# A fourth staging buffer for weights, and gates that keep the scaled projection in the place of their result

## The chip, the cores and the metric

The kernel runs on one core of a Trainium2 chip. The core has five engines that work side by side, each through its own instructions in order: TensorE (PE in the profile; its weight loads are shown apart as PEld), VectorE (DVE), ScalarE (ACT), GpSimd (POOL) and SyncE (SP, which here only issues transfers). The metric is the device time of one execution in microseconds. Three runs of the kernel before took 1794.14, 1794.47 and 1795.31 us; their median is 1794.47.

## The reference

The kernel computes two layers of a decoder trunk on 512 tokens of width 2048, in float32. A layer normalises its input, multiplies it by one wide matrix, runs three groups of heads on the parts of the product, gates each with a SiLU, and multiplies the result by an output matrix, onto the residual.

```
def _layer(x, norm_g, w_in, ..., w_out):
    h = _rmsnorm(x, norm_g)
    proj = h @ w_in                      # 2048 x 7696
    (cv_h, cv_b, cv_c, cv_g, sb_q, sb_k, sb_v, sb_g,
     gl_q, gl_k, gl_v, gl_g, gl_lr) = split(proj)
    y_conv = cv_b * (conv3(cv_c * cv_h) + bias) * silu(cv_g)          # 512 columns
    y_sb   = stick_breaking(rms(sb_q), rms(sb_k), sb_v) * silu(sb_g)  # 8 heads of 128
    g      = log_sigmoid(gl_lr @ gla_w_up + gla_b_up) / 16
    y_gla  = rms(gla(gl_q, gl_k, gl_v, g)) * silu(gl_g)               # 4 heads
    return x + concat(y_conv, y_sb, y_gla) @ w_out                    # 2048 x 2048
```

`stick_breaking` is a causal attention of which the weights come from sums of log-sigmoids over the keys; `gla` is a linear attention whose state decays by a gate that depends on the data.

## The kernel before

**Weights in blocks.** Both matrices are cut into blocks of 256 columns (one has 16 columns more, the low-rank part). There are 38 blocks a layer: 30 of `w_in`, then 8 of `w_out`. The list `specs` has them in the order of use. Each block is loaded in two halves of 1024 rows (the contraction dimension). A half goes through these steps:

- `fetch` (L295): SyncE issues a 1 MB transfer into a staging tile of the pool `stage`, which has three buffers. For the block with the low-rank part there is a second, small transfer.
- `wmax` (L306): ScalarE squares the staged half and sums it, for a bound on its size. The squares go into a scratch tile, `junk`.
- `wscale` (L313 to L329), once for a block: GpSimd adds the two halves' sums over the partitions, and VectorE makes a power of two of them.
- `whi` (L343): ScalarE writes the scaled half as float16, the high part, into the tile `wh` of the pool `wpool`, three buffers.
- `wlo` (L350): VectorE writes what the high part left over, also in float16, into `wl`. It is the last reader of the staging tile, so its end gives the buffer back.

A projection is three products of float16 parts: high times high, high times low and low times high. There are three forms. `project_cols` (L507 to L509) puts columns on the partitions, 96 matmuls of 128x512. `project_toks` (L515 to L517) puts tokens there, 192 matmuls of 128x256. `project_by_token` (L540) does one group of tokens after another, each with all high parts first and the low part of the weights last; it is used where each group of tokens is wanted by itself, at the two ends of a layer. A projection writes two of the three PSUM banks of the pool `psp`.

**Order of the work.** In a layer: the values of the linear attention (blocks 0 and 1, by token), its query and key, its two gates, the first convolution half (four blocks, of which the third is its gate), four rounds of attention heads (value, gate, query, key), the second convolution half, and the output projection. The linear attention's levels (L673 to L723) and its output (L766 to L798) run beside the convolution's and the first attention round's projections. An attention round's scores and values are put into a list, `later`, and taken out of it between the projections of the next round: the weights of the heads (tile `za`) are turned by transposing transfers (L911, issued by SyncE) into the tile `th`, and L927 multiplies them by the values.

The program is traced in this order, with the loads of the next block (`load`, called by `weights` for the block in use and the one after) at a higher priority. A planner then orders the instructions of each engine by an estimated timeline, and gives out the buffers of the pools as they come free in it. So a load is placed where its staging buffer is free in that timeline, however early that is. At the start of the kernel the order on VectorE and ScalarE is written out by hand.

**The gates.** `gate` (L546 to L560) makes a SiLU of two PSUM banks, one after the other. ScalarE copies the scaled bank (L550) into the scratch tile `gy`, of which there is one; then comes a chain of ScalarE and VectorE steps on a second scratch tile `ga` (L552 to L556, two buffers); and VectorE multiplies both into the gate's tile `g` (L557). `g` has two buffers. They go to the two gates of the linear attention (last read at L798), the two of the convolution and the four of the attention rounds (last read at L934); at the end of layer 0 also to the gain of the next norm.

Two more places use `gy`: the column numbers `colno` in the startup (L107 to L124), and a scratch tile `r_` of the decay (L624 to L626).

Of the kernel before, what the change touches and what calls it, by code (L numbers as in the profile page):

```python
# [11 lines left out]
ALU = mybir.AluOpType  # L12
# [5 lines left out]
P = 128  # L18
# [16 lines left out]
def hybrid_trunk(ctx, tc, x, norm_g, w_in, conv_w, conv_b, sb_qn_g, sb_kn_g,  # L35
                 gla_w_up, gla_b_up, gla_on_g, w_out, out):
    nc = tc.nc
    V, S, G, T = nc.vector, nc.scalar, nc.gpsimd, nc.tensor
    depth, D = norm_g.shape
    seq = x.shape[1]  # L40
# [6 lines left out]
    NG = D // GW  # L47

    const = ctx.enter_context(tc.tile_pool(name="const", bufs=1))
    stage = ctx.enter_context(tc.tile_pool(name="stage", bufs=3))  # L50
    wpool = ctx.enter_context(tc.tile_pool(name="wpool", bufs=3))
    big = ctx.enter_context(tc.tile_pool(name="big", bufs=4))
    work = ctx.enter_context(tc.tile_pool(name="work", bufs=2))
# [8 lines left out]
    def nm(s):  # L62
        uid[0] += 1
        return f"{s}_{uid[0]}"
# [4 lines left out]
    def wk(shape, tag, bufs=None, dt=F32):  # L69
        return work.tile(shape, dt, tag=tag, name=nm(tag), bufs=bufs)  # L70
# [4 lines left out]
    def bank(pool, tag):  # L75
        return pool.tile([P, 512], F32, tag=tag, name=nm("ps" + tag))
# [27 lines left out]
    epst = const.tile([P, 1], F32, tag="epst", name="epst")  # L104
    V.memset(epst, EPS)

    colno = wk([P, P], "gy", 1)  # L107
    V.tensor_tensor_scan(colno, ones.to_broadcast([P, P]), ones.to_broadcast([P, P]), -1.0, ALU.mult, ALU.add)
    parno = wk([P, 32], "raw", 1)
    V.transpose(parno, colno[:, :32])  # L110
# [380 lines left out]
    for l in range(depth):  # L491
# [53 lines left out]
        def gate(ps, u, mx=None):  # L545

            g = wk([P, 2, seq], "g")
            for c in range(2):
                y = wk([P, seq], "gy", 1)
                S.activation(y, ps[c], AF.Copy, scale=u)  # L550
                a = wk([P, seq], "ga")
                S.activation(a, y, AF.Abs)  # L552
                S.activation(a, a, AF.Exp, scale=-1.0)
                S.activation(a, a, AF.Ln, bias=1.0)
                V.scalar_tensor_tensor(a, y, 0.0, a, ALU.min, ALU.subtract)
                S.activation(a, a, AF.Exp)  # L556
                V.tensor_tensor(g[:, c, :], y, a, ALU.mult)  # L557
            if mx is not None:
                V.tensor_reduce(mx, g, AX.XY, ALU.max, apply_absolute_value=True)
            return g  # L560
# [55 lines left out]
        for p in range(2):  # L616
            gp = bank(psm, "m")
            T.matmul(gp, wup[:, p * P:(p + 1) * P], lrT, start=True, stop=True)
            bcol = par[:, base["bu"] + 2 * l + p:base["bu"] + 2 * l + p + 1]
            a = wk([P, seq], "ga")  # L620
            S.activation(a, gp, AF.Abs, bias=bcol)
            S.activation(a, a, AF.Exp, scale=-1.0)
            S.activation(a, a, AF.Ln, bias=1.0)
            r_ = wk([P, seq], "gy", 1)  # L624
            S.activation(r_, gp, AF.Relu, bias=nbu[:, l, p:p + 1], scale=-1.0)
            V.tensor_tensor(a, a, r_, ALU.add)  # L626
            for t in range(NT):
                ts_ = slice(t * P, (t + 1) * P)
                V.tensor_tensor_scan(Pc[:, p, ts_], ones.to_broadcast([P, P]), a[:, ts_], 0.0, ALU.mult, ALU.add)
# [32 lines left out]
        for p in range(2):  # L662
            ps, u = project_cols()
            gmx = sm(1, "ggm")
            gg.append(gate(ps, u, gmx))
            m = sm(1, "gb")
            V.tensor_tensor(m, gmx, onmax[:, l:l + 1], ALU.mult)
            gsc.append(mixscale(6 + p, m, "g"))
# [23 lines left out]
        for p in range(2):  # L692
# [88 lines left out]
            for hh in range(2):  # L781
# [8 lines left out]
                r_ = wk([P, seq], "e")  # L790
# [46 lines left out]
        def conv_out(j, y, then=lambda: None):  # L837

            ps, u = project_cols()
            g = gate(ps, u)  # L840
            V.tensor_tensor(y, y, g, ALU.mult)
            bound = sm(2, "cm")

            def limit(m):
                V.tensor_reduce(m, y, AX.XY, ALU.max, apply_absolute_value=True)
                return m

            then()
            if j:

                V.tensor_scalar(bound[:, 1:2], limit(bound[:, 0:1]), loaded[cursor[0]][1], 2.0 ** 29, ALU.mult, ALU.mult)
                s_ = mixscale(j, bound[:, 1:2], "c", 14.0)
                weight_ratio()
            ps, u = project_cols()
            for c in range(2):
                V.scalar_tensor_tensor(y[:, c, :], ps[c], u, y[:, c, :], ALU.mult, ALU.mult)
            if not j:
                s_ = mixscale(j, limit(bound[:, 0:1]), "c")
            for c in range(2):
                mixsplit(2 * j + c, y[:, c, :], s_)  # L860
# [80 lines left out]
        for j in range(4):  # L941
# [14 lines left out]
            go()  # L956
            ps, u = project_cols()
            g = gate(ps, u, bm[:, 1:2])
            gm = allmax(bm[:, 0:1], 1, "b")
            m = sm(1, "sbm")  # L960
# [109 lines left out]
```

## Time and profile before

| | |
|---|---|
| median of three runs | 1794.47 us |
| the profiled execution | 1794.15 us |
| its span in the profile | 1792.4 us |
| TensorE busy | 1746.4 us, 97% of the span |
| ScalarE busy | 1090.8 us, 61% |
| VectorE busy | 1040.0 us, 58% |
| mean granted TensorE clock | 0.997 |
| weights and other data moved | 202.62 MB, 113 GB/s |

All times within the profile are microseconds from the start of the span. A row of the timeline has the start, the duration, the engine (SPq is SyncE's queue), the line, the operation, the tiles written and read, and in brackets the idle time of the engine before it and who ended it. A row of waits has the engine and line that waited and the one waited for; then the sum in us, the number of times and the longest. A row of windows has the stretch and its length, then busy time and number of instructions of PE, PEld, DVE, ACT and POOL (fewer columns where one line alone is asked for), the granted clock as a share of full speed, the DMA engines' busy share and the GB/s they moved. A row of transfers has the tiles, the queue, the kind, the number, the size of each, and the median time from issue to landing. The ends of matmuls are modelled, so that a busy TensorE is not one at its peak.

### The profile page before, as it was taken

The page shows a single profiled execution, that of the slowest core. Times are in us where ns is not written, and L with a number is a line of the kernel's source. Part 1 is how long each engine was busy: PE and PEld are TensorE (multiplying, and loading weights), DVE is VectorE, ACT ScalarE, POOL GpSimd, SP SyncE. Part 2 cuts the span into 40 slices and gives each one's busy share as a digit, 9 for nine tenths or more (in the row PEclk, how much of TensorE's full clock was granted, in tenths as well). Part 3 has the DMA queues.
Part 4 walks back from the last instruction along what each step waited for, and adds up shares of the span by engine and source line. Part 5 has one row for each costly group of instructions (what it writes and reads, how often), then busy time and mean ns, then how long its engine had stood idle before and what let it go on. Part 6 is the DMA issues. An engine that isn't in the chain of part 4 may idle for free. (4 is left out here: it accounts for less than half of the span.)

```text
span 1792.4 us, 30839 instructions
## 1 busy us (share of the span) xinstructions
PE 1746.4 (97%) x12880; PEld 1238.9 (69%) x12880; DVE 1040.0 (58%) x1977; ACT 1090.8 (61%) x1655; POOL 54.9 (3%) x105
## 2 busy tenths in 40 slices
PE   7999999999999999999999999999999999999999
PEld 5744446777778764788886444568686878548888
DVE  5466777656565656533464575876666566564333
ACT  8557566667575766555554675665666666665431
POOL 1000000000000000000010000000000000000000
PEclk9999999999999999999999999999999999999999
DMA  6322222243535344454423232223444534444441
GB/s 216 118 95 94 71 94 72 92 121 86 141 102 133 109 128 115 143 178 142 134 82 118 94 93 73 80 86 83 132 111 114 128 107 124 119 123 142 142 142 48
DMA packets 257676, 202.62 MB, mean 113 GB/s; under 512 B 84658, under 2 KB 256764, under 8 KB 257024
## 3 DMA queue, kind: packets, MB, share of 16 engines
q1 hardware_dynamic: 248528, 191.19, 37.0%
q10 hardware_dynamic: 9008, 9.45, 1.6%
q8 instruction: 101, 1.65, 0.4%
q14 instruction: 39, 0.32, 0.1%
HBM read 173.36 MB, written 8.39 MB: 101 GB/s over the span
## 5 line engine op out<-in xcount | busy, mean ns | idle before, releaser
L306 ACT ACTIVATE junk<-st 128x2048 uint8<-128x2048 f32 (+1 forms) x152 | 291.0, 1914 | 334.6 <-DMA st<-in_w_in_dram 240.1
L515 PE MATMUL psp<-wh,m 128*128 128x256 f16 x1664 | 453.6, 273 | 2.6 <-DVE raw L981 1.7
L517 PE MATMUL psp<-wh,m 128*128 128x256 f16 x1664 | 453.5, 273 | 0.0
L516 PE MATMUL psp<-wl,m 128*128 128x256 f16 x1664 | 453.5, 273 | 0.0
L350 DVE SCALAR_TENSOR_TENSOR wl<-st,ws,wh 128x2048 f16<-128x2048 f32 (+1 forms) x120 | 282.1, 2353 | 153.3 <-ACT wh L343 145.9
L343 ACT ACTIVATE wh<-st,ws 128x2048 f16<-128x2048 f32 (+1 forms) x120 | 239.8, 2000 | 92.1 <-PE psp L517 58.0
L515 PE MATMUL psp<-wh,x 128*128 128x256 f16 x768 | 209.9, 273 | 2.3 <-DVE raw L981 1.7
L516 PE MATMUL psp<-wl,x 128*128 128x256 f16 x768 | 209.9, 273 | 0.0
L517 PE MATMUL psp<-wh,x 128*128 128x256 f16 x768 | 209.8, 273 | 0.0
L507 PE MATMUL psp<-x,wh 128*128 128x512 f16 x512 | 194.1, 379 | 0.0
L507 PE MATMUL psp<-m,wh 128*128 128x512 f16 x512 | 194.1, 379 | 0.0
L508 PE MATMUL psp<-x,wh 128*128 128x512 f16 x512 | 194.0, 379 | 0.0
L508 PE MATMUL psp<-m,wh 128*128 128x512 f16 x512 | 194.0, 379 | 0.0
L509 PE MATMUL psp<-x,wl 128*128 128x512 f16 x512 | 193.7, 379 | 0.0
L509 PE MATMUL psp<-m,wl 128*128 128x512 f16 x512 | 193.7, 379 | 0.0
L509 PEld LDWEIGHTS <-wl 128*128 128x128 f16 x1024 | 100.2, 98 | 123.0 <-issue 4.4
L508 PEld LDWEIGHTS <-wh 128*128 128x128 f16 x1024 | 100.2, 98 | 117.4 <-issue 2.1
L507 PEld LDWEIGHTS <-wh 128*128 128x128 f16 x1024 | 100.2, 98 | 117.1 <-issue 2.0
L515 PEld LDWEIGHTS <-m 128*128 128x128 f16 x1664 | 162.8, 98 | 23.9 <-DVE raw L981 2.3
L516 PEld LDWEIGHTS <-m 128*128 128x128 f16 x1664 | 162.8, 98 | 20.5 <-issue 1.6
L517 PEld LDWEIGHTS <-m 128*128 128x128 f16 x1664 | 162.8, 98 | 20.1 <-issue 1.4
L316 DVE TENSOR_SCALAR wq<-wgm 128x1 f32<-128x1 f32 x76 | 16.2, 213 | 262.1 <-POOL wgm L313 262.0
(267 smaller groups left out, 2315.9 us busy)
## 6 DMA issues: line engine op xcount, KB each, us to landing
st<-in_w_in_dram SPq DMA_DIRECT2D x120, 1024.0 KB, 5.3
st<-in_w_out_dram SPq DMA_DIRECT2D x32, 1024.0 KB, 5.8
x<-in_x_dram SPq DMA_DIRECT2D x4, 1024.0 KB
qT<-in_x_dram ACTq DMA_DIRECT2D x8, 512.0 KB, 5.1
qT<-xs ACTq DMA_DIRECT2D x8, 512.0 KB
xs<-x SPq DMA_DIRECT2D x14, 256.0 KB, 4.4
out_dram<-kT SPq DMA_DIRECT2D x14, 256.0 KB, 4.3
th<-za SPq DMA_TRANSPOSE x64, 5.5
```

The lines of the kernel that those rows point to most:

```text
L306: S.activation(junk(HK * n).rearrange("p (k n) -> p k n", k=HK), staged[i][h][:, :, :n], AF.Square, accum_out=peak[i][:, h:h + 1])
L316: V.tensor_scalar(m, gm[:, 0:1], gm[:, 1:2], 2.0 ** -120, ALU.add, ALU.max)
L343: S.activation(wh[:, ks, :n], staged[i][h][:, ks, :n], AF.Copy, scale=s_)
L350: V.scalar_tensor_tensor(wl[:, ks, :n], staged[i][h][:, ks, :n], s_, wh[:, ks, :n], ALU.mult, ALU.subtract)
L507: T.matmul(o, wh[:, kk, cs], xh[:, :, k, :], start=st_, stop=False)
L508: T.matmul(o, wh[:, kk, cs], xl[:, :, k, :], start=False, stop=False)
L509: T.matmul(o, wl[:, kk, cs], xh[:, :, k, :], start=False, stop=en)
L515: T.matmul(o, ah[:, t, k, :], wh[:, kk, :n], start=st_, stop=False, skip_group_check=True)
L516: T.matmul(o, ah[:, t, k, :], wl[:, kk, :n], start=False, stop=False, skip_group_check=True)
L517: T.matmul(o, al[:, t, k, :], wh[:, kk, :n], start=False, stop=en, skip_group_check=True)
```

## The change

The pool `stage` gets a fourth buffer. A staging tile is 8 x 272 float32 on each partition, 8704 bytes. The tag `gy` (one tile of 512 float32, 2048 bytes a partition) goes away, and its three users move:

- In `gate` the scaled bank is copied into the half of `g` where the result will stand, and the last product is made in place.
- The column numbers take a buffer of the tag `th`, the turned attention weights.
- The decay's scratch takes a buffer of the tag `za`, the attention weights before they are turned.

```
-    stage = ctx.enter_context(tc.tile_pool(name="stage", bufs=3))
+    stage = ctx.enter_context(tc.tile_pool(name="stage", bufs=4))
...
-    colno = wk([P, P], "gy", 1)
+    colno = wk([P, P], "th", 2)
...
             g = wk([P, 2, seq], "g")
             for c in range(2):
-                y = wk([P, seq], "gy", 1)
+                y = g[:, c, :]
                 S.activation(y, ps[c], AF.Copy, scale=u)
                 a = wk([P, seq], "ga")
...
                 S.activation(a, a, AF.Exp)
-                V.tensor_tensor(g[:, c, :], y, a, ALU.mult)
+                V.tensor_tensor(y, y, a, ALU.mult)
...
-            r_ = wk([P, seq], "gy", 1)
+            r_ = wk([P, seq], "za")
```

## The prediction

> **What bounds the kernel now.** I read the page's first two parts, then TensorE's waits, then every stretch in which TensorE waited, on all engines.
>
> ```profile
> span 1792.4 us, 30839 instructions
> PE 1746.4 (97%) x12880; PEld 1238.9 (69%) x12880; DVE 1040.0 (58%) x1977; ACT 1090.8 (61%) x1655; POOL 54.9 (3%) x105
> ```
> ```profile
> PE psz L688 <- ACT m L682: 5.3, 11, 1.3
> PE psm L927 <- DMA th<-za: 5.0, 6, 2.3
> PE psz L779 <- ACT za L766: 4.9, 4, 1.7
> PE psp L540 <- ACT wh L343: 4.9, 2, 3.4
> ```
> ```profile
> ACT junk L306 <- DMA st<-in_w_in_dram: 240.1, 90, 8.4
> SPq L295 <- DVE wl L350: 831.4, 103, 19.7
> ACT gy L550 <- DVE g L557: 3.9, 2, 2.1
> ```
>
> TensorE is the bound: it is idle for 1792.4 - 1746.4 = 46 us, in waits of which, the startup aside, only one is over 2.3 us. Its weights come late at one line only, L540 (4.9 us, two waits, one of them 3.4). So the 831 us that SyncE spends waiting for a staging slot (L350 frees it) are no loss by themselves. They matter where ScalarE, which works in the order of its queue, stands before a load that has not landed: L306 does so for 240 us. Most of that is idle time that ScalarE has to spare; it costs only where TensorE needs what stands behind it in the queue. The gates' single scratch tile shows in 3.9 us, two waits.
>
> The run that was profiled took 1794.15 us, 1.75 over its span and 0.32 under the median 1794.47; I make the sum against 1794.15 and add 0.32 at the end.
>
> **Fourth staging buffer, at the start of layer 1.** This is the place where a slot is worth time. SyncE, ScalarE, VectorE, TensorE in turn:
>
> ```profile
> 875.24 3.98 SPq L295 DMA_DIRECT2D st<-in_w_in_dram  x3
> 898.14 1.00 SPq L295 DMA_DIRECT2D st<-in_w_in_dram  x2
> 914.89 0.38 SPq L295 DMA_DIRECT2D st<-in_w_in_dram  x1
> 929.78 15.34 SPq L295 DMA_DIRECT2D st<-in_w_in_dram  x3
> ```
> ```profile
> 914.00 1.02 ACT L410 ACTIVATE m<-psz 128x1024 f16<-128x1024 f32 x1 [4.17 <-PE psz L408]
> 916.98 2.02 ACT L306 ACTIVATE junk<-st 128x2176 uint8<-128x2176 f32 x1
> 919.44 2.00 ACT L306 ACTIVATE junk<-st 128x2176 uint8<-128x2176 f32 x1
> 924.59 2.10 ACT L343 ACTIVATE wh<-st,ws 128x2176 f16<-128x2176 f32 x1
> 935.62 1.91 ACT L306 ACTIVATE junk<-st 128x2048 uint8<-128x2048 f32 x1 [5.71 <-DMA st<-in_w_in_dram]
> 937.53 2.09 ACT L343 ACTIVATE wh<-st,ws 128x2176 f16<-128x2176 f32 x1
> ```
> ```profile
> 927.28 2.47 DVE L350 SCALAR_TENSOR_TENSOR wl<-st,ws,wh 128x2176 f16<-128x2176 f32 x1
> ```
> ```profile
> 929.05 5.52 PE L540 MATMUL psp<-wh,m 128*128 128x256 f16 x48 [0.24 <-ACT m L410]
> 935.93 0.38 PE L540 MATMUL psp<-wl,m 128*128 128x256 f16 x2
> 939.67 0.61 PE L540 MATMUL psp<-wh,m 128*128 128x272 f16 x2 [3.35 <-ACT wh L343]
> ```
> ```profile
> 939.70:945.44 5.74, 5.74 (x26) 3.75 (x26) 5.03 (x3) 2.08 (x2) 0.00 (x0) 0.50 0.36 108
> 450.49:453.92 3.43, 2.83 (x13) 1.89 (x14) 2.27 (x4) 1.06 (x1) 0.00 (x0) 0.50 0.90 251
> ```
>
> The second half of block 1's high part (L343 at 937.53) needs a buffer that block 0 last reads in the matmuls ending at 929.05 + 5.52 = 934.57. It starts 937.53 - 934.57 = 3 us later, because a squaring pass (L306 at 935.62) stands ahead of it and waits 5.71 us for a load. That load was issued at 929.78, when L350 (927.28 + 2.47 = 929.75) gave its slot back. TensorE ran out at 935.93 + 0.38 = 936.31 and waited 3.35 us; after that its clock was granted at half for 5.74 us more, 2.87 us of work lost.
>
> With four slots each load takes the slot freed one half earlier. The second half of block 1, issued at 898.14, goes out with the group at 875.24; its squaring passes, at 916.98 and 919.44, fit into ScalarE's 4.17 us of idle time before 914.00 or earlier; the high part at 924.59 and the low part at 927.28 move up with them, and so does the load that they release. The squaring pass that blocked is then done before 934.57, the high part runs from there for 2.09 us to 936.7, and TensorE waits 936.7 - 936.3 = 0.4 us. The gain is 3.35 - 0.4 = 2.95 of wait and 2.87 of clock: **5.8 us**. Ends: 0, if another load takes that place, and 3.35 + 2.87 = 6.2. I take 5.8, since the chain moves up by 921.44 - 914.00 = 7.4 us or more (the end of the second squaring, now and then), and 937.53 - 934.57 = 3 us are needed.
>
> [...]
>
> **Fourth staging buffer, elsewhere.** The same transfers, squarings and conversions are issued, so no work is added or removed. In the steady state the pace of the loads is set by TensorE: it frees a buffer of converted weights, L343 and L350 convert, L350 frees a slot, L295 fetches, L306 squares. A fourth slot moves this row one half ahead and leaves as many squarings behind a fresh load as before. I take 0. The lower end is that the waits at L779 (4.9) and L927 (5.0), where ScalarE had just stood at L306, all go, with the half clock after 450 (3.43 x 0.5 = 1.7): -11.6.
>
> ```profile
> 0.00:44.80 44.80, 34.85 (x202) 24.42 (x203) 26.07 (x82) 37.36 (x44) 7.09 (x12) 1.00 0.65 216
> ```
> ```profile
> st<-in_w_in_dram SPq DMA_DIRECT2D x120, 1024.0 KB, 5.3
> th<-za SPq DMA_TRANSPOSE x64, 5.5
> ```
>
> In the startup, the second half of layer 0's block 1 can now be fetched before the small parameter rows. The slice moved 216 GB/s at 0.65 busy, so 332 when busy, and one half more (1024 KB, 1.05 MB) ahead of the rows is 3.2 us. That is the upper end if TensorE stood still for the transpose of those rows. I take 0, the nearest row being the startup's own order, in which nothing waits for them: the planner puts that transpose where it sees the rows arrive.
>
> **The gates write into their result.** No instruction is added: the same copy and the same product, at other addresses. What changes is waits, and they bind at one gate, that of the first convolution half (layer 0 shown, and one row of layer 1).
>
> ```profile
> 240.01 0.67 ACT L550 ACTIVATE gy<-psp,wu 128x512 f32<-128x512 f32 x1
> 252.02 0.69 ACT L550 ACTIVATE gy<-psp,wu 128x512 f32<-128x512 f32 x1 [2.06 <-DVE g L557]
> 264.66 0.63 ACT L556 ACTIVATE ga<-ga 128x512 f32<-128x512 f32 x1 [2.07 <-DVE ga L555]
> ```
> ```profile
> 247.65 0.74 DVE L798 SCALAR_TENSOR_TENSOR za<-za,par,g 128x512 f32<-128x512 f32 x1
> ```
> ```profile
> 266.39 0.22 PE L688 MATMUL psz<-m 128*128 128x128 f16 x1 [0.51 <-ACT m L682]
> 267.58 0.22 PE L688 MATMUL psz<-m 128*128 128x128 f16 x1 [0.64 <-ACT m L682]
> 1152.51 0.22 PE L688 MATMUL psz<-m 128*128 128x128 f16 x1 [0.52 <-ACT m L682]
> ```
> ```profile
> 248.00:265.06 17.06, 9.10 (x24) 2.32 (x24) 1.00 0.22 67
> ```
>
> Gained: the second copy (252.02) need not wait for the first half's product, so the chain behind it is over before 264.66, where it now holds ScalarE for 2.07 us, and the two waits at 266.39 and 267.58 (1.15 us) may go. Twice, for the same in layer 1 (0.52 at 1152.51 is its first): -2.3. Lost: the first copy (240.01) now needs a gate tile. There are two, and one is read last at 247.65 + 0.74 = 248.39. So the PSUM bank is free at 248.39 + 0.67 = 249.1 instead of 240.7. The next projection (32 matmuls of L507; the last row counts the 24 after its first 8) enters its second bank at 248.0: 1.1 us of wait, 2.2 in two layers. Since ScalarE no longer runs the gate at 240, L798 can also come earlier, and then it is 0. Ends -2.3 and +2.2; I take 0. At the other gates both tiles are long free.
>
> **Index tile and decay scratch.** They move into tags with two buffers of which the first use comes hundreds of us later or earlier; the work that hides them is all of the first projections. 0.
>
> **Sum:** 1794.15 - 5.8 + 0 + 0 = 1788.35, and 0.32 for the median: **1788.7 us**.
>
> **Rivals.**
> 1. *The waits at loads go everywhere.* By -11.6 more: 1777. For it: ScalarE's idle time at L306 stands before the waits at L779 and L927. Against: the pace argument above. [...]
> 2. *The change does not do what it says.* A later load takes the place of the one at 935.62, and the wait stays: 1794.5. Against: the blocks ahead are converted 7 us sooner, and 3 are enough.
> 3. *Transposes queue behind loads: slower.*
>
> ```profile
> 449.48 4.89 SPq L911 DMA_TRANSPOSE th<-za  x3
> ```
>
> Attention's transposes (5.5 us to landing) share SyncE's queue with the loads, and six times TensorE already waits for them at L927. If a slot that is free earlier puts one more megabyte ahead of each, each of the six grows by 3.2 us: 1788.7 + 19 = 1808. It decides from (5.8 + 3.6) / 6 = 1.6 us each on, 3.6 being what can be told. Against: one load per freed slot, as before.
> 4. *The gate tile's wait is real and cools the clock.* At 248.0 a wait of 2 us (the 1.1, and as much again for what ScalarE has in hand by then) and 1.7 us of half clock, in both layers: 1788.7 + 7.4 = 1796, or 1802 where the gain at 936 fails too.
>
> **Chances.** Forecast 0.36, with a range of its own of 1785 to 1791; rival 1 0.11; rival 2 0.15; rival 3 0.23; rival 4 0.15, of which a third stays within 0.2% (3.6 us, about what a measurement of this kernel can tell). Faster 0.36 + 0.11 = 0.47; same 0.15 + 0.05 = 0.20; slower 0.23 + 0.10 = 0.33. The planner writes a new order for the whole program when slots change; that is why rivals 3 and 4 have as much as they have. The range reaches from rival 1 to just short of rival 3, 1777 to 1806, and leaves out about half of each.
>
> **What the new profile would show.** Right: no wait over 1 us at L540 near 936 and no half clock after it; squarings of layer 1's block 1 before 914; the second copy of the first convolution's gate following the first without a product between; L306's idle total about as before. Wrong: L927's waits longer than 5.0 in sum, a new wait of L507 on L550, a wait in the first 45 us at the parameter rows, or L688's waits for L682 well over 5.3 us in sum because the new order suits the gated linear attention less well.

## The result, and the profile after

The changed kernel takes 1801.64 us (median of four runs, 1800.52 to 1804.52), the kernel before 1794.31 us (four runs, 1793.05 to 1795.31): 1.0037 times as long, with a 95% interval of 1.0022 to 1.0052. It was forecast 5.8 us faster and is about 7 us slower. The profiled execution took 1800.52 us, 6.37 more than the one before; its span is 6.3 us longer. (A later run of the kernel before took 2604.4 us at a granted clock of 0.657; it is left out of the ratios.)

The page's span, TensorE's share of it and the transposing transfers:

```profile
span 1798.7 us, 30845 instructions
...
PE 1749.3 (97%) x12880; PEld 1241.2 (69%) x12880; DVE 1036.6 (58%) x1977; ACT 1092.5 (61%) x1655; POOL 55.1 (3%) x105
...
th<-za SPq DMA_TRANSPOSE x64, 3.7
```

TensorE's waits after the change, in us: the total, how often, the longest.

```profile
PE psp L515 <- DVE raw L981: 15.5, 7, 2.9
PE psm L789 <- ACT e L787: 6.1, 4, 2.1
...
PE psp L540 <- ACT wh L343: 2.0, 2, 1.6
PE psp L540 <- ACT m L410: 1.7, 1, 1.7
...
PE psp L507 <- ACT g L550: 1.0, 1, 1.0
```

The same view of the kernel before, its rows that the prediction had no use for:

```profile
PE psp L515 <- DVE raw L981: 3.4, 6, 0.6
...
PE psz L779 <- DVE e L767: 3.2, 2, 1.6
...
PE psz L779 <- DVE za L767: 0.9, 2, 0.5
...
PE psm L789 <- ACT e L787: 0.3, 1, 0.3
```

The rows that this view lists add up to 41.9 us before and 45.4 after, 3.5 more. What moved most:

| wait of TensorE | before | after | difference |
|---|---|---|---|
| key projection, second bank, for the query normalisation (L515 <- L981) | 3.4 | 15.5 | +12.1 |
| linear attention's mean square (L789 <- L787) | 0.3 | 6.1 | +5.8 |
| linear attention's output (L779, its three rows) | 9.0 | none | -9.0 |
| attention's values for the transposes (L927) | 5.0 | none | -5.0 |
| projection by token for weights (L540 <- L343) | 4.9 | 2.0 | -2.9 |
| projection by token for the turned activations (L540 <- L410) | 0.2 | 1.7 | +1.5 |

The other part is the clock. Before, the trace shows it granted at half in two stretches (3.41 us from 450.5 and 6.83 us from 938.6); after, in five of 3.41 us (from 325.5, 448.4, 544.0, 639.5 and 1523.6). At the granted 0.50 at most half of the time is lost, 10.24 / 2 = 5.1 us before and 17.05 / 2 = 8.5 after; it is less where TensorE also waits within the stretch. The busy times have it as it is: TensorE is busy for 1749.3 us after and 1746.4 before, 2.9 more, and idle for 49.4 and 46.0, 3.4 more. Together these are the 6.3 us of the span.

At the place for which the gain was forecast, the wait for weights is gone. TensorE and ScalarE at the start of layer 1, after the change:

```profile
928.56 1.09 PE L408 MATMUL psz<-ident,x 128*128 128x128 f32 x8 [0.57 <-DVE m L417]
931.33 2.79 PE L540 MATMUL psp<-wh,m 128*128 128x256 f16 x24 [1.67 <-ACT m L410]
...
935.70 1.91 PE L540 MATMUL psp<-wl,m 128*128 128x256 f16 x16
937.45 2.71 PE L540 MATMUL psp<-wh,m 128*128 128x272 f16 x23
```
```profile
919.01 2.02 ACT L306 ACTIVATE junk<-st 128x2176 uint8<-128x2176 f32 x1
...
921.21 2.00 ACT L306 ACTIVATE junk<-st 128x2176 uint8<-128x2176 f32 x1
...
928.37 1.90 ACT L306 ACTIVATE junk<-st 128x2048 uint8<-128x2048 f32 x1
...
930.26 1.01 ACT L410 ACTIVATE m<-psz 128x1024 f16<-128x1024 f32 x1
```

Block 1's squaring passes stand at 919.01 and 921.21. The changed kernel reaches layer 1 5.3 us later, so on the clock of before they stand at 913.7 and 915.9, against 916.98 and 919.44: 3.3 and 3.5 us earlier. The second half's high part (L343, now at 940.09) waits 1.51 us for TensorE to give its buffer back, and no longer behind a load. Block 1's first matmuls (the row with 128x272, which also counts some of block 0 that stand between them) follow with no wait, and no half clock comes after them. New is the wait of 1.67 us at 931.33. The copy L410 that it needs ends at 930.26 + 1.01 = 931.27. The transposes that it copies end at 928.56 + 1.09 = 929.65, so 1.0 us of the wait is the copy itself; 0.6 is the squaring pass in front of it (it ends at 928.37 + 1.90 = 930.27), of a load that now lands sooner.

Counted by the matmuls of the projections, 192 to a block, the changed kernel is 5.3 us behind at the start of layer 1 (914.7 against 909.4), 7.5 behind 192 matmuls later (941.9 against 934.4) and 1.2 behind after 192 more (964.4 against 963.2). So 2.2 us are lost and 6.3 gained, 4.1 in all, against a forecast of 5.8. No half clock comes with the two new waits here (0.57 us at L408, 1.67 at L540; the clock is granted at 1.00 from 900 to 960). The six other traces with four buffers, below, have the same two (0.5 to 0.6 and 1.7 us), and in four of them (`after_bank` and the three with both edits) 3.41 us of half clock come with them, from 921.5, 919.2, 921.3 and 918.1.

The loss is in the attention rounds. Round 2 of layer 0 after the change, TensorE, ScalarE and VectorE (an idle time before an instruction, and what ended it, stand in brackets):

```profile
540.59 0.27 PE L515 MATMUL psp<-wh,x 128*128 128x256 f16 x1
543.05 0.27 PE L515 MATMUL psp<-wh,x 128*128 128x256 f16 x1 [2.19 <-DVE raw L981]
```
```profile
537.67 0.28 ACT L972 ACTIVATE raw<-psp 128x128 f32<-128x128 f32 x1
...
537.92 1.92 ACT L306 ACTIVATE junk<-st 128x2048 uint8<-128x2048 f32 x1
...
539.82 0.72 ACT L586 ACTIVATE m<-e,bsmix 128x512 f16<-128x512 f32 x1
540.43 0.39 ACT L182 ACTIVATE qr<-qs,epst,qu 128x8 f32<-128x8 f32 x1
```
```profile
542.22 1.29 DVE L981 TENSOR_TENSOR raw<-psp,qr 128x512 f32<-128x512 f32 x2
```

And the same round before:

```profile
543.03 0.27 PE L517 MATMUL psp<-wh,x 128*128 128x256 f16 x1
543.50 0.27 PE L927 MATMUL psm<-th,v 128*128 128x256 f16 x1 [0.20 <-DMA th<-za]
544.37 0.28 PE L515 MATMUL psp<-wh,x 128*128 128x256 f16 x1 [0.59 <-DVE raw L981]
```
```profile
533.45 1.91 ACT L306 ACTIVATE junk<-st 128x2048 uint8<-128x2048 f32 x1 [6.34 <-DMA st<-in_w_in_dram]
```
```profile
543.62 1.29 DVE L981 TENSOR_TENSOR raw<-psp,qr 128x512 f32<-128x512 f32 x2
```

A projection by tokens writes two banks, and `psp` has three. So the key projection's first bank is free, while its second is the one from which the query normalisation (L981) still reads. The key projection starts at 531.75 after and at 532.66 before (the first L515 of each). L981 starts 542.22 - 531.75 = 10.5 us into it after, and 543.62 - 532.66 = 11.0 before: it is half a microsecond earlier, not later. But the order of TensorE has changed. Before, all 96 matmuls of the first bank stand ahead of the second one's first, 10.5 us at 0.109 us from one to the next; after, 82 do, 8.9 us, and the other 14 stand behind the wait (counted in the traces). It is so in rounds 1 to 3 of both layers; the seventh wait, 1.3 us, is in round 0 of layer 1, with 78 ahead. Where the gap was 1.3 us from the last matmul of the first bank to the first of the second (543.03 to 544.37, with one of L927 in it), it is now 2.46 (540.59 to 543.05), and a stretch of half clock follows from 544.0 on:

```profile
544.00:547.41 3.41, 3.41 (x18) 2.42 (x17) 0.00 (x0) 2.27 (x3) 0.00 (x0) 0.50 0.12 43
```

The squaring pass (L306) that a freed slot feeds has moved too. Before, it stands early, at 533.45, in idle time; now it stands at 537.92 between the queries' squares (L972) and their logarithm (L182), with 1.9 us, and the logarithm waits for it.

### The profile page after: what moved, and what is told of

The parts are those of the page before. It is cut to its first block, busy times and chain, and to the rows that moved or that the text cites. A ratio compares the mean times of both kernels' runs of the same rounds, so it can differ in the third digit from the quotient of the medians.

```text
span 1798.7 us, 30845 instructions
## 1 busy us (share of the span) xinstructions
PE 1749.3 (97%) x12880; PEld 1241.2 (69%) x12880; DVE 1036.6 (58%) x1977; ACT 1092.5 (61%) x1655; POOL 55.1 (3%) x105
## 5 line engine op out<-in xcount | busy, mean ns | idle before, releaser
L515 PE MATMUL psp<-wh,m 128*128 128x256 f16 x1664 | 454.1, 273 | 8.2 <-DVE raw L981 8.2
L306 ACT ACTIVATE junk<-st 128x2048 uint8<-128x2048 f32 (+1 forms) x152 | 291.2, 1916 | 271.0 <-DMA st<-in_w_in_dram 198.9
L343 ACT ACTIVATE wh<-st,ws 128x2048 f16<-128x2048 f32 (+1 forms) x120 | 239.6, 2000 | 117.7 <-PE psp L517 75.1
L515 PE MATMUL psp<-wh,x 128*128 128x256 f16 x768 | 211.9, 276 | 7.4 <-DVE raw L981 7.4
L507 PE MATMUL psp<-m,wh 128*128 128x512 f16 x512 | 194.0, 379 | 1.0 <-ACT g L550 1.0
L507 PE MATMUL psp<-x,wh 128*128 128x512 f16 x512 | 194.0, 379 | 0.0
L515 PEld LDWEIGHTS <-m 128*128 128x128 f16 x1664 | 163.1, 98 | 29.1 <-issue 9.9
L507 PEld LDWEIGHTS <-wh 128*128 128x128 f16 x1024 | 100.2, 98 | 120.0 <-issue 4.2
```

The source lines that it names most:

```text
L306: S.activation(junk(HK * n).rearrange("p (k n) -> p k n", k=HK), staged[i][h][:, :, :n], AF.Square, accum_out=peak[i][:, h:h + 1])
L343: S.activation(wh[:, ks, :n], staged[i][h][:, ks, :n], AF.Copy, scale=s_)
L507: T.matmul(o, wh[:, kk, cs], xh[:, :, k, :], start=st_, stop=False)
L515: T.matmul(o, ah[:, t, k, :], wh[:, kk, :n], start=st_, stop=False, skip_group_check=True)
```

## The experiments

Two theories came out of this. **P**: the loss is the place of the key projection's second bank, 14 matmuls too early. **Q**: it is the squaring pass inside the query normalisation. First, though, which half of the change carries the loss.

**Each half alone.** `slots_only` has four staging buffers with `gy` kept. The room for it comes from the small scratch tiles that are used once, which get one buffer each in place of several:

```
-    stage = ctx.enter_context(tc.tile_pool(name="stage", bufs=3))
+    stage = ctx.enter_context(tc.tile_pool(name="stage", bufs=4))
...
-        return small.tile([P, n], F32, tag=tag, name=nm(tag), bufs=bufs)
+        return small.tile([P, n], F32, tag=tag, name=nm(tag), bufs=1 if tag in ONCE else bufs)
```

> Four staging buffers, with the gates' scratch tile gy kept as before (its 2 KB come from 26 small tiles of which only one is live at a time and which get one buffer instead of two; with three staging buffers that alone leaves the order on every engine as it was). Theory S, the slots carry both the gain and the loss: the wait at L540 near 936 us and its half clock are gone (-6 us), the second half of the key projection waits for the query's normalisation (L515 for L981) 14 us or more in sum against 4.5 before, with half clock after some of them; time 1799 to 1803. Theory G, the gates carry the loss: L515's waits stay at 4 to 5 us and the time is 1786 to 1790.

`gates_only` has the edits of the gate, `colno` and `r_`, and three staging buffers.

> Three staging buffers, the gates, the index tile and the decay scratch as in the change. Theory S: the wait at L540 near 936 us stays at 3 us or more with its half clock, L515's waits for L981 stay below 7 us in sum, time 1791 to 1797. Theory G: L515's waits for L981 are 14 us or more, the wait near 936 stays too, time 1804 to 1810.

Measured: `slots_only` 1802.2 us, 1.0046 times the kernel before (1.0032 to 1.0060); `gates_only` 1794.7, 1.0007 times (0.9995 to 1.0018). (No run has the single buffers of the small tiles without the fourth slot.) TensorE's waits in `slots_only`, then in `gates_only`:

```profile
PE psp L515 <- DVE raw L981: 14.3, 6, 3.0
...
PE psm L789 <- ACT e L787: 6.3, 4, 2.2
...
PE psp L540 <- ACT wh L343: 1.8, 2, 1.4
```
```profile
PE psm L789 <- ACT e L787: 6.7, 4, 2.6
PE psp L540 <- ACT wh L343: 6.2, 3, 3.4
...
PE psp L515 <- DVE raw L981: 4.4, 8, 0.6
```

The slots carry both sides: the wait for weights at L540 falls and that for L981 rises with them alone. The gates' edit is worth nothing that can be told. The wait at L789 comes with either half, and `gates_only`, which has it too, is not slower: by itself it does not make the loss.

**The loss put into the kernel before.** In `before_81` TensorE starts the second bank after 81 matmuls of the first in those six rounds; 15 follow. The order on all other engines is that of the kernel before.

```
+            steps = [(t, k) for b in range(2) for ks in rounds for t in (...) for k in ks]
+            if split: steps.insert(split, steps.pop(32))
...
+                with (tc.issue_after(mark.ins) if split and split < n_ < 33 else ExitStack()): one = tok_mm(...)
+                if n_ == split: mark = one
...
-                ps, u = project_toks(xh, xl)
+                ps, u = project_toks(xh, xl, split=27 if gain is not None and j else 0)
```

> The kernel before with one thing moved: in rounds 1 to 3 of the attention of both layers, TensorE starts the second bank of the key projection after 81 of the first bank's 96 matmuls; the other 15 follow it. The order on VectorE, ScalarE, GpSimd and SyncE is that of the kernel before. Theory P (the loss of the change is the second bank's early place, since it waits for the query normalisation, L981): each of the six waits of L515 for L981 grows by 15 x 0.109 = 1.6 us, 9.8 us in all, and four or more of them, now 3 us and longer, are followed by half clock at 1.7 us each: 1802 to 1814 us, the likeliest 1808. Rival (the place does not matter: the matmuls behind the wait are late either way, or the loss comes from the loads and the vector engines of four slots): 1793 to 1796.

Measured: 1812.4 us, 1.0094 times the kernel before (1.0081 to 1.0107; that one took 1795.61 on this chip). Its waits, and the round shown above:

```profile
PE psm L927 <- DMA th<-za: 15.9, 6, 3.9
...
PE psp L515 <- DVE raw L981: 3.3, 6, 0.6
```
```profile
545.56 0.27 PE L517 MATMUL psp<-wh,x 128*128 128x256 f16 x1
547.88 0.27 PE L927 MATMUL psm<-th,v 128*128 128x256 f16 x1 [2.05 <-DMA th<-za]
548.74 0.28 PE L515 MATMUL psp<-wh,x 128*128 128x256 f16 x1 [0.59 <-DVE raw L981]
```

The size is as expected: the two waits add up to 19.2 us, against 8.4 before, so 10.8 more, where 9.8 were expected. The trace shows half clock after five of the six gaps; the mean granted clock is 0.992 over the run, against 0.997 in the kernel before. The place is not quite as expected: L927 stands in the queue between the two banks here, and it takes the longer wait; that for L981 follows. The 15 matmuls were the cover of both. The instructions of the other engines stand in the same order in the two traces. So 15 matmuls in each of six rounds, 90 of 12880, moved behind these waits, cost 1812.4 - 1795.6 = 16.8 us, half clock included.

**The cover put back into the changed kernel.** `after_bank` writes the key projection bank by bank:

```
-            for ks in rounds:
-                for t in range(NT):
+            for ks, t in [(ks, t) for b in range(2) for ks in rounds for t in (2 * b, 2 * b + 1)] if banked else [...]:
...
-                ps, u = project_toks(xh, xl)
+                ps, u = project_toks(xh, xl, banked=gain is not None)
```

> The changed kernel, with the key projection written bank by bank (all 96 matmuls of the first bank, then the second), in all rounds. Theory P: with 96 in place of 82 matmuls ahead, the six waits of L515 for L981 fall by 14 x 0.109 = 1.5 us each, that of round 0 of layer 1 (78 ahead) goes: about 10.6 us; and what is left of each, 0.6 to 1.4 us, is too short for the half clock seen after four of them, at 1.7 us each: 1784 to 1791, so faster than both kernels. Rival (the loss of four slots lies in loads or in the vector engines, and the wait moves to the next reader of the bank): 1799 to 1803.

Measured: 1790.53 us, 0.9977 times the kernel before (0.9964 to 0.9991).

```profile
PE psp L515 <- DVE raw L981: 5.5, 6, 1.6
...
PE psp L515 <- DVE raw L989: 3.9, 4, 1.6
```
```profile
538.47 0.27 PE L515 MATMUL psp<-wh,x 128*128 128x256 f16 x1 [0.79 <-DVE raw L981]
```

The wait falls from 15.5 to 5.5 us, as expected, and the trace shows no half clock in the attention rounds (mean granted clock 0.999 over the run, 0.995 in the changed kernel). Part of it, 3.9 us, goes to the next reader of the bank (L989, the key normalisation). L981 ends no sooner in the round than in the changed kernel (11.2 us after the projection's start in both). So the place of the second bank makes the loss, and with the cover restored the kernel with four slots is a little faster than the kernel before. The place of 14 matmuls a round turned the sign. (In these rounds of the kernel before, all 96 stand ahead already.)

**The squaring pass taken out of the normalisation.** `after_squares` puts the loads that are traced two blocks later behind the exponential of the query normalisation (L183) on ScalarE:

```
-                load(j)
+                with (tc.issue_after(behind[i]) if behind.get(i) is not None else ExitStack()): load(j)
...
-                rsqrt(rs, sq, u2, 8, "q")
+                nrm = rsqrt(rs, sq, u2, 8, "q"); behind[cursor[0] + 1] = (nrm.ins if gain is None else None)
```

> The changed kernel, with the squaring passes (L306) of the weights that are loaded two blocks ahead put behind the query normalisation's exponential (L183) on ScalarE; in the changed kernel one of 1.9 us stands between the squares of the queries (L972) and their logarithm (L182). Theory Q (that pass is what makes the normalisation late): L981 ends at about 9.3 us after the key projection's start instead of 11.2. The planner then puts only 72 matmuls, 7.9 us, ahead of the second bank, so a wait of about 1.5 us stays in each of the six rounds in place of 2.3 to 3.2, without half clock: 1786 to 1793. Theory P alone (only the count of matmuls matters): the wait grows by 10 x 0.109 = 1.1 us each and the time to 1806 or more. Rival (neither): 1799 to 1803.

Measured: 1796.88 us, 1.0008 times the kernel before (0.9997 to 1.0019). That is a miss for theory Q as it was put (1786 to 1793), but not for the pass as a cause. The same round:

```profile
538.22 0.39 ACT L182 ACTIVATE qr<-qs,epst,qu 128x8 f32<-128x8 f32 x1
538.64 0.21 ACT L183 ACTIVATE qr<-qr 128x8 f32<-128x8 f32 x1
538.76 1.89 ACT L306 ACTIVATE junk<-st 128x2048 uint8<-128x2048 f32 x1
```
```profile
539.13 0.74 DVE L587 SCALAR_TENSOR_TENSOR m<-e,bsmix,m 128x512 f16<-128x512 f32 x1
...
540.66 1.29 DVE L981 TENSOR_TENSOR raw<-psp,qr 128x512 f32<-128x512 f32 x2
```
```profile
541.50 0.27 PE L515 MATMUL psp<-wh,x 128*128 128x256 f16 x1 [2.03 <-DVE raw L981]
```

L182 stands 2.2 us earlier than in the changed kernel. L981 is earlier by 1.6 by the clock of the trace and by 1.3 from the start of the projection, because VectorE finishes L587 first. TensorE gets only part of it: the new order has 72 matmuls ahead of the second bank in place of 82, 1.1 us fewer, and the wait stays (13.6 us in all against 15.5), with half clock in four stretches where the changed kernel has five (mean granted clock 0.996 against 0.995). Against that kernel's 1.0037, the edit is still worth 0.3%, some 5 us.

**Both edits, with four slots and with three.** `after_both` has the two edits in the changed kernel.

> The changed kernel with both edits: the key projection bank by bank, and the squaring passes behind the query normalisation. If the two causes add up (theories P and Q), 96 matmuls take 10.5 us and the normalisation ends at about 9.3: no wait of L515 for L981 is left, against 15.5 us in the changed kernel, and no half clock follows: 1777 to 1784. If the wait passes to the next reader, or the delayed squaring passes make weights late: 1788 to 1800.

Measured: 1777.04 us, 0.990 times the kernel before (0.9887 to 0.9914). The view of everything that waits for L981 over the whole run is empty:

```profile
L981 DVE TENSOR_TENSOR raw<-psp,qr x16: 678/686/692, 353.4 to 1505.6; 128x512 f32<-128x512 f32 x16
...
who waited for it (us, times):
```

Against the changed kernel's 1.0037 the first edit alone is worth 0.6% and the second 0.3%; the two together are worth 1.4%, more than the sum. Whether the fourth buffer has a part in that, the same edits in the kernel before tell; the pair was run on two more chips.

> The kernel before (three staging buffers, the gates' own buffer) with the two edits of after_both: the key projection bank by bank, and the squaring passes behind the query normalisation. It tells whether the fourth buffer is worth anything once its loss is gone. If it is (the boundary wait of 3.4 us and its half clock near 939 us stay here): the waits of L515 for L981, 3.4 us, go, and the half clock at 450 us, 1.7 us: about 1789 to 1792, 10 us or more above after_both. If the gain of after_both lay in the two edits alone: 1776 to 1782.

> The kernel of after_both once more, on the chip of before_both, for the difference of the two. By the earlier run 1777, from 1775 to 1781. If four slots are worth their gain at the boundary alone (6.3 us less 2.2 us of new waits, and 2 us of load waits), it lies 5 to 12 us under before_both; if not, within 2 us of it.

> The kernel of before_both once more, beside after_both_c on one chip. In the pair before, on a chip on which the kernel before took 1805 us, the two had the same time (1789.3 and 1788.8), though their profiled executions lay 7.6 us apart. If the fourth buffer is worth its boundary gain: 1785 to 1790, 5 us or more above after_both_c. If two edits bring all of it: within 2 us of after_both_c.

> As before_both_c, with four buffers. If the fourth buffer is worth its boundary gain: 1775 to 1782; if not, within 2 us of before_both_c, wherever that lies.

| chip | kernel before | both edits, three slots | both edits, four slots |
|---|---|---|---|
| of `before_both` | 1804.67 | 1789.25, 0.9913 (0.9889 to 0.9938) | 1788.75, 0.9913 (0.9891 to 0.9934) |
| of `before_both_c` | 1799.45 | 1786.79, 0.9930 (0.9915 to 0.9946) | 1781.23, 0.9894 (0.9879 to 0.9909) |

Most of the gain is in the two edits, which are worth 12.7 to 15.4 us to the kernel before as well. With them that kernel's waits at L927 (5.0 us) are gone, and of its waits for L981 (3.4) 1.5 us are left in `before_both` and 0.6 in `before_both_c`. The fourth slot adds 0.5 us on one chip and 5.6 on the other, where the times do not overlap (1783.08 to 1790.75 against 1780.67 to 1781.87). By its expectation, the first pair says that the fourth buffer is worth nothing once the edits are in, and the second that it is worth its gain at the boundary. In the profiled executions of the second pair the boundary wait (3.1 us) is there with three slots and not with four, where the two waits left for L343 are in the startup:

```profile
PE psp L540 <- ACT wh L343: 4.6, 2, 3.1
```
```profile
PE psm L789 <- ACT e L787: 6.5, 4, 2.3
...
PE psp L540 <- ACT wh L343: 2.0, 2, 1.6
PE psp L540 <- ACT m L410: 1.7, 1, 1.7
```

They show what takes it back too: L410 at the boundary and L789 in the linear attention. Half clock at the boundary is no gain either in this pair: 3.41 us with three slots and with four. Why the first pair shows nothing of the fourth buffer stays open. Against the kernel before, four slots with both edits are the fastest version on one chip, and level with three on the other.

## Why the prediction was wrong, step by step

- **Start of layer 1: right in its mechanism, 4.1 us in place of 5.8.** The wait of 3.35 us and the 6.83 us of half clock went, 6.3 us gained. The chain moved up by 3.3 to 3.5 us and not by "7.4 us or more", which was just enough for the 3 that were needed. What the step left out are the 2.2 us of new waits just ahead, of which 0.6 is a squaring pass that moved up in front of L410. It asked only whether the loads come early enough, not whom they push back. No half clock came with the new waits, where four other traces have 3.41 us of it. The half clock after the old wait is no fixed price either: in the traces with three slots it lasts 6.83 us in `before` and `before_both`, and 3.41 in `gates_only`, `before_81` and `before_both_c`, after a wait of 3.1 to 3.4 us each time. At 3.41 us, so 1.7 of work lost, the step's sum gives 2.95 + 1.7, some 4.7, no worse a forecast than 5.8.
- **Fourth staging buffer, elsewhere, "I take 0": the step that failed.** Its sentence "no work is added or removed" is true, and its lower end came nearly as written: the waits at L779 (9.0 with its other two rows) and at L927 (5.0) are gone. But that part of the sum had no upper end. The order that the planner wrote for the new buffer puts the key projection's second bank behind 82 in place of 96 matmuls (+12.1 us of waits), and brings half clock after four of the attention waits (2.19 to 2.88 us), where it was one (2.27), and after a wait at L789 (2.07). The wait at L789 (+5.8) came as L779's went, and the gates' edit brings it as well. `before_81` and `after_bank` show that the place of the second bank decides the sign. The pace argument, by which a slot "leaves as many squarings behind a fresh load as before", does not hold either. ScalarE's waits for loads fell from 240.1 us to 198.9, and a pass that had stood in idle time came to stand in the query normalisation:

```profile
ACT junk L306 <- DMA st<-in_w_in_dram: 198.9, 81, 6.4
```

- **The startup, taken as 0: a small cost.** The changed kernel is 1.5 us behind at the fifth block (123.4 against 121.9), inside the stated 0 to 3.2. No experiment looked at it.
- **The gates, taken as 0: right in the sum, by moves that it did not name.** `gates_only` shows 1.0007 (0.9995 to 1.0018), in which L779's waits fall from 9.0 to 4.2 us and L789's rise from 0.3 to 6.7. Of the wait behind rival 4 (L507 for L550) there is one, 1.0 us, in the changed kernel, and the clock stays at 1.00 around it.
- **Rival 3, transposes behind loads: wrong in its mechanism.** They land in 3.7 us where it was 5.5, and L927 waits no more. The kernel is slower all the same, by another way.
- **Rival 2, the wait at the boundary stays: wrong.** It went.
- **The chances** named the planner's new order as the reason for what was given to slower, but no rival was an order that sheds its cover. The profile of before had a sign of it: the wait for L981 was there six times, at most 0.6 us, at the same place in each round, and L927's six waits stood just ahead of it. A wait that short and that regular is one that the order only just covers.

## What to carry to other kernels

Where a planner writes the order, one more buffer need not be a local change: look for the waits of the old profile that recur, short, at one place in a loop, count the work that covers each of them, and price what the loss of a few instructions of cover would cost times the rounds. If the cover matters, write it into the program (here, one bank after the other) so that an estimate a microsecond off cannot take it away. And shortening the chain that is waited for may give less than it should, when the new order places the waiting work earlier (`after_squares`, 0.3%); shorten it and fix the order together (1.4%).

## What the runs showed of the hardware

The length of a wait alone did not decide whether half clock came with it. These are all of TensorE's waits of 1.8 us or more after the first 25 us in the profiled executions of the two kernels; the clock is granted at 0.50 in each stretch and at 1.00 before and after it:

| kernel | wait of TensorE, us | ends at | half clock |
|---|---|---|---|
| before | 2.27 (L927 for the transposes) | 450.59 | 3.41 us from 450.5 |
| before | 3.35 (L540 for L343) | 939.67 | 6.83 us from 938.6 |
| after | 2.07 (L789 for L787) | 325.21 | 3.41 us from 325.5 |
| after | 2.29 (L515 for L981) | 448.52 | 3.41 us from 448.4 |
| after | 2.19 (L515 for L981) | 543.05 | 3.41 us from 544.0 |
| after | 2.88 (L515 for L981) | 638.36 | 3.41 us from 639.5 |
| after | 1.90 (L789 for L787) | 1213.30 | none |
| after | 2.36 (L515 for L981) | 1336.42 | none |
| after | 2.08 (L515 for L981) | 1429.25 | none |
| after | 2.46 (L515 for L981) | 1522.47 | 3.41 us from 1523.6 |

A wait of 2.07 us has half clock behind it and one of 2.36 has none. Each stretch of 3.41 us costs at most 1.7 us, half of it. The two waits at the start of layer 1 (0.57 and 1.67 us in the changed kernel), with which half clock came in four traces of seven, are shorter than any of these. What decides, these runs do not show; so a forecast of a new wait of some 2 us in this kernel has 0 and 1.7 us as the ends of what the clock adds.

The same kernel also differs from set to set of runs: the kernel before took medians of 1793.81, 1794.31, 1795.61, 1799.45 and 1804.67 us in five sets, of which the four of the experiments were on four chips, a spread of 0.6%, more than the effect under study. With one set on each chip, no run tells the chip from the time of the set. Only ratios to runs of the same set can be compared.
